# Delta-rule tiles in a pool of their own, three early expert loads, and transposes one chunk later

## The chip, the cores and the metric

The kernel runs on one core of a Trainium2 chip. The metric is the device time of one execution in microseconds (us). Five engines work from queues of their own, each in the order that was fixed when the program was built: TensorE (PE: matmuls and transposes), VectorE (DVE), ScalarE (ACT), GpSimd (POOL) and SyncE (SP, which issues all loads of weights). They meet at semaphores: an instruction waits until what it reads is there and what it overwrites is no longer used.

## The reference

Two layers over 256 tokens of width 1024, in fp32. Each layer has a mixer of three branches, whose outputs are joined and projected back, and a feed-forward part, dense in layer 0 and a mixture of experts in layer 1:

```python
for layer in range(DEPTH):                     # 2
    h = rmsnorm(x, mix_norm[layer])
    (c_q, c_kv, k_rope, lru_x, lru_gate, g_q, g_k, g_v, g_z, g_a, g_b) = jnp.split(h @ w_in[layer], split_at, axis=-1)
    y_mla = mla_mixer(...)      # 4 heads, attention by chunks, causal over chunks of 64
    y_lru = rglru_mixer(...)    # gated linear recurrence, 512 channels
    y_gdn = gdn_mixer(...)      # gated delta rule, 4 heads of 128, chunks of 64 with a triangular solve
    x = x + jnp.concatenate([y_mla, y_lru, y_gdn], axis=-1) @ w_out[layer]
    h = rmsnorm(x, ffn_norm[layer])
    if layer % 2 == 0:
        x = x + swiglu(h, ...)                 # width 2816
    else:
        x = x + moe_swiglu(h, ...)             # 8 experts of width 3584, the best 2 for each token
```

## The kernel before, in words

**Precision.** A weight is split into a high part `h` (a copy on ACT, line 271) and a low part `l` (the difference on DVE, line 272), and a product is three matmuls: high by high, high by low, low by high (`mm3`). All matmuls and transposes are issued by one helper, line 119, so that the profile tells them apart by the tiles: `mm` are projections, `gd` products of the mixers, `tp` transposes, `gu` the experts' gate and up products, `py` their down products. Inverse square roots are an addition on DVE (line 195) and a power on POOL (line 196).

**The mixer.** `mixer(l)` holds one generator for each part of the work: `gdn_in` and `gdn` (delta rule), `lru_in` and `lru_out`, `mla_in`, `mla_qkv` (queries, keys, values), `attn`, `zgate`, `gdn_out`, `wo0` to `wo2` (output projection, added into the residual at line 485). A table written by hand, `PLAN`, says in which order they advance by a step; a step with `!` is pinned ahead of what follows. A scheduler then orders each engine's instructions within these bounds, by what is free and ready in its own model. All tiles of the mixer come from one pool, `mix`, which is closed by the step `free`, near the end of the table. The delta rule's tiles are `cb` (convolution input), `v2k`, `aad` and `aao` (decay masks), `nbm`, `p128` and the small `qi`, `pi`, `vi`; `cb` and `p128` are cleared by memsets on POOL (lines 517 and 611). The last reader of the masks is the matmul `gd<-g2k,aad`.

**The loads.** `load` issues one transfer of 1 MB on SP. Its buffer comes from a ring of 128 x 2048 tiles: five in the pool `rawp` and, in layer 1 from `free` on, six in a second one, `raw2`. While the string `HEAD` lasts, a load takes its place from there: one letter a load, `2` the second pool, `1` the first, `h`, `q` and `g` tiles that at this time lie idle (high and low parts, hidden tiles). `rawi` counts on around the ring; its starting value says which buffer is taken first when the string is used up:

```python
HEAD = "hhq222222111ggg11"
...
raw_pools[:] = ring2
rawi[0] = len(ring2)
head[:] = () if again else list(HEAD)
```

**The experts.** After the routing, tokens are gathered into slots: five experts have 64 slots (narrow: raw fp32 matmuls, no split) and three have 128 (wide: split weights). Each has seven groups of 512 hidden channels, and a group has four loads of gate and up weights (`mgu`) and two of down weights (`mdn`). Groups are chained in software: while the `gu` products of one group run, the hidden tile of the group before (`esg`: SiLU on ACT, line 1369, times up on DVE, line 1370) is transposed (`tp`) and multiplied down (`py`). Narrow and wide groups alternate over long stretches, and in nine narrow groups the transposes of the own hidden tile stand directly behind the 32 `gu` matmuls, ahead of `py`. A narrow group multiplies four chunks of eight matmuls; in `gate_up` the function `mid` issues the transposes after the second.

## Time and profile before

| what | value |
|---|---|
| median of three runs | 1464.56 us |
| lowest, highest | 1463.25, 1467.42 us |
| profiled execution, time | 1467.6 us |
| its span in the trace | 1465.8 us |
| mean granted TensorE clock | 0.986 |
| layer 0: mixer, dense part | 0 to 200, 200 to 411 us |
| layer 1: mixer, routing, experts | 411 to 614, 614 to 631, 631 to 1466 us |

The profiled execution is one run by itself: what lies around its span is 1.8 us, and it is 3.0 us over the median, so differences of durations in the trace are set against its own time and then carried to the median. A row of the timeline gives the start, the length, the engine, the line, the operation, what it writes and reads, and in brackets how long its engine stood idle ahead of it and what ended that. `x4` joins four such instructions in one row.

### The profile page before, as it was taken

How to read it: one execution, taken by the hardware profiler on the slowest of the kernel's cores; microseconds unless marked ns; L12 is line 12 of the kernel's file. 1: busy time of each engine (PE TensorE's matmuls, PEld its weight loads, DVE VectorE, ACT ScalarE, POOL GpSimd, SP SyncE). 2: the span in 40 equal slices, each digit the busy share in tenths (PEclk: the TensorE clock that was granted, in tenths of full speed). 3: DMA queues.
4: the chain of work that ended last, by engine and by line, in shares of the span. 5: the costliest groups of instructions: out<-in, count | busy, mean ns of one | idle time of the engine just before them, and what ended most of it. 6: DMA issues, size and time to landing. Idle time of an engine off the chain costs nothing.

```text
span 1465.8 us, 25644 instructions
## 1 busy us (share of the span) xinstructions
PE 1407.3 (96%) x10407; PEld 1093.5 (75%) x10407; DVE 842.4 (57%) x1250; ACT 680.7 (46%) x1059; POOL 98.2 (7%) x122
## 2 busy tenths in 40 slices
PE   6989999999999999999999999999999999999996
PEld 6988799999999887966666666656665656666663
DVE  7898676666568985644353535454534545364542
ACT  5655654444456657354352535243533434343430
POOL 1111201221011121000000000000000000000000
PEclk9999999999999999999999999999999999999998
DMA  6422336544544132889999999999999999999993
GB/s 247 146 88 101 116 115 231 175 174 159 187 173 173 60 115 102 347 347 391 425 426 426 425 426 425 426 425 426 426 425 421 424 422 426 425 409 426 425 426 156
DMA packets 63773, 442.96 MB, mean 302 GB/s; under 512 B 7200, under 2 KB 7456, under 8 KB 11936
## 3 DMA queue, kind: packets, MB, share of 16 engines
q1 hardware_dynamic: 63360, 441.01, 74.6%
q8 instruction: 83, 1.36, 0.4%
q10 hardware_dynamic: 288, 0.25, 0.1%
q14 instruction: 42, 0.34, 0.1%
HBM read 440.18 MB, written 1.05 MB: 301 GB/s over the span
## 4 chain that ended last, share of the span: by engine, by line
PE 87%; DVE 7%; issue 2%; ACT 2%; POOL 1%; DMA 0%; POOLq 0%; DVEq 0%; ACTq 0%
PE gu L119 34%; PE mm L119 19%; PE py L119 17%; PE gd L119 11%; PE tp L119 7%; DVE l L272 2%; DVE red L369 1%; POOL so L196 0%; ACT h L271 0%; DVE xl L350 0%; DMA raw<-prm 0%; DVE esg L1370 0%; ACT esg L1369 0%; DVE acc L1437 0%; ACT m4k L759 0%
## 5 line engine op out<-in xcount | busy, mean ns | idle before, releaser
L272 DVE TENSOR_TENSOR l<-raw,h 128x1024 fp32r<-128x1024 f32 x416 | 491.8, 1217 | 101.2 <-ACT h L271 100.0
L271 ACT ACTIVATE h<-raw 128x1024 fp32r<-128x1024 f32 x416 | 421.1, 1048 | 169.9 <-PE mm L119 81.0
L119 PE MATMUL gu<-raw,y 128*64 128x256 f32 x2160 | 251.9, 382 | 0.0
L119 PE MATMUL gu<-h,y 128*128 128x512 f32 (+1 forms) x704 | 222.0, 401 | 0.0
L119 PEld LDWEIGHTS gu<-raw,y 128*64 128x64 f32 x2160 | 151.3, 137 | 87.3 <-issue 16.5
L119 PE MATMUL mm<-xh,h 128*128 128x256 f32 (+1 forms) x672 | 193.6, 288 | 9.3 <-ACT h L271 9.3
L119 PE MATMUL mm<-xh,l 128*128 128x256 f32 (+1 forms) x672 | 193.4, 288 | 0.8 <-DVE l L272 0.8
L119 PE MATMUL mm<-xl,h 128*128 128x256 f32 (+1 forms) x672 | 193.3, 288 | 0.2 <-issue 0.2
L119 PEld LDWEIGHTS gu<-h,y 128*128 128x128 f32 (+1 forms) x704 | 129.2, 187 | 38.7 <-ACT h L271 6.5
L119 PE MATMUL gu<-l,y 128*128 128x512 f32 (+1 forms) x368 | 137.3, 396 | 1.7 <-DVE l L272 1.7
L119 PEld LDWEIGHTS mm<-xh,h 128*128 128x128 f32 (+1 forms) x672 | 128.5, 191 | 10.2 <-ACT h L271 9.3
L119 PEld LDWEIGHTS mm<-xh,l 128*128 128x128 f32 (+1 forms) x672 | 128.5, 191 | 1.9 <-DVE l L272 1.3
L119 PEld LDWEIGHTS mm<-xl,h 128*128 128x128 f32 (+1 forms) x672 | 128.6, 191 | 1.4 <-issue 0.7
L119 PE MATMUL py<-raw,htn 128*64 128x512 f32 x552 | 126.7, 598 | 0.0
L1370 DVE SCALAR_TENSOR_TENSOR esg<-gu,rs,esg 128x256 f32<-128x256 f32 x35 | 16.9, 484 | 146.9 <-ACT esg L1369 146.9
L1396 ACT ACTIVATE hth<-tp 128x512 fp32r<-128x512 f32 x21 | 12.5, 597 | 189.3 <-PE tp L119 189.3
L119 PEld LDWEIGHTS py<-raw,htn 128*64 128x64 f32 x552 | 37.0, 136 | 68.5 <-issue 66.3
L1369 ACT ACTIVATE esg<-gu,rs 128x256 f32<-128x256 f32 x35 | 16.6, 474 | 150.9 <-PE gu L119 150.9
L119 PEld LDWEIGHTS gu<-l,y 128*128 128x128 f32 (+1 forms) x368 | 66.0, 186 | 18.6 <-DVE l L272 2.7
L119 PE MATMUL mm<-y,h 128*128 128x256 f32 x384 | 70.2, 284 | 0.0
L119 PE MATMUL py<-l,hth 128*128 128x512 f32 x168 | 68.5, 408 | 1.2 <-DVE l L272 1.2
L1383 DVE SCALAR_TENSOR_TENSOR esg<-gu,rs,esg 128x512 f32<-128x512 f32 x21 | 15.8, 750 | 91.0 <-PE gu L119 91.0
(391 smaller groups left out, 2057.1 us busy)
## 6 DMA issues: line engine op xcount, KB each, us to landing
raw<-mgu SPq DMA_DIRECT2D x219, 1024.0 KB, 13.0
raw<-mdn SPq DMA_DIRECT2D x110, 1024.0 KB, 12.6
raw<-win SPq DMA_DIRECT2D x29, 1024.0 KB, 4.9
raw<-dgu SPq DMA_DIRECT2D x22, 1024.0 KB, 4.9
raw<-wout SPq DMA_DIRECT2D x12, 1024.0 KB, 4.8
raw<-ddn SPq DMA_DIRECT2D x8, 1024.0 KB, 4.9
raw<-ddn SPq DMA_DIRECT2D x4, 768.0 KB, 4.2
raw<-uqn SPq DMA_DIRECT2D x2, 1024.0 KB, 4.8
```

The costliest lines, as they stand in the source:

```text
L119: i = f(*a, **k)
L271: SC.activation(h[:, c], w, AF.Copy)
L272: V.tensor_tensor(out=lo[:, c], in0=w, in1=h[:, c].bitcast(F32), op=ALU.subtract)
L369: V.tensor_reduce(out=red, in_=sqv.rearrange("p k t -> p t k"), axis=AX.X, op=ALU.add)
L1369: keep(SC.activation(sg, ps[:, :256], AF.Silu, scale=rs))
L1370: keep(V.scalar_tensor_tensor(sg, ps[:, 256:], rs, sg, ALU.mult, ALU.mult))
L1383: keep(V.scalar_tensor_tensor(sg, ps[1], rs, sg, ALU.mult, ALU.mult))
L1396: keep(SC.activation(hth, pt, AF.Copy))
```

## The change

Three edits, and the diff's core. First, the delta rule's tiles are taken from a pool of their own, `gdp`, on the right side of the on-chip memory. It is closed when the generator `gdn` ends, long before `free`. Second, in layer 1 the room is given at that moment to a pool `raw3` of three load buffers, and the first three loads of expert 0 are issued (`pre`); `raw2` has three buffers instead of six, the ring keeps its eleven and `HEAD` its seventeen loads in another order, and `rawi` starts so that the first three places behind the string are `rawp` buffers. Third, in a narrow group `mid` stands after the third chunk.

```diff
-RAW2 = 6
+RAW2 = 3
+RAW3 = 3
-HEAD = "hhq222222111ggg11"
+HEAD = "333222hqh111ggg11"
...
+        def open_raw3():
+
+            pools["3"] = top.enter_context(tc.tile_pool(name="raw3", bufs=RAW3, side="right")), "raw3"
+            head[:] = HEAD[:RAW3]
+            for hf in range(RAW3):
+                pre.append(load(A["mgu"][0, 0, hf // 2, hf % 2]))
+
...
-            ring2[:] = [(rawp, "raw") if x == "1" else (raw2, "raw2") for x in HEAD if x in "12"]
+            pools["2"] = raw2, "raw2"
+            ring2[:] = [pools[x] for x in HEAD if x in pools]
...
+                st_g = st.enter_context(ExitStack())
+                gdp = st_g.enter_context(tc.tile_pool(name=f"gdp{l}", bufs=1, side="right"))
+
...
-                        cb = mp.tile([P, 2, S + 3], F32, tag="cb", name=nm("cb"), bufs=2)
+                        cb = gdp.tile([P, 2, S + 3], F32, tag="cb", name=nm("cb"), bufs=2)
...
-                    aad = mk(mp, [P, NT, HEADS, 2, P], F32, "aad")
-                    aao = mk(mp, [P, HEADS, 2, P], F32, "aao")
+                    aad = mk(gdp, [P, NT, HEADS, 2, P], F32, "aad")
+                    aao = mk(gdp, [P, HEADS, 2, P], F32, "aao")
...
-                    P128 = mk(mp, [P, NS, P], F32, "p128")
+                    P128 = mk(gdp, [P, NS, P], F32, "p128")
...
+                            if name == "gdn":
+                                st_g.close()
+                                if l == DEPTH - 1:
+                                    open_raw3()
...
-                        rawi[0] = len(ring2)
-
-                        head[:] = () if again else list(HEAD)
+                        rawi[0] = 2 * len(ring2) - sum(x in pools for x in head)
+
+                        head[:] = () if again else HEAD[RAW3:]
...
-                                    if m == 0:
-                                        mid()
+                                        if m > hf:
+                                            mid()
...
-                                for half in load(weights(name, i, *at), nk * cols, halves):
+                                for half in pre.pop(0) if pre else load(weights(name, i, *at), nk * cols, halves):
```

Since the tiles' places differ, the scheduler gives another order in layer 1's mixer too, though `PLAN` is the same. In the rows below, a tile's number is its running number in the program.

**PE at the end of the attention (585 to 593 us).** Here `t2k_7063` (`t2k_7080` after the change) is the attention's output, whose four transposes follow a chain over ACT, DVE and POOL; the last product ahead of that chain is `gd_7054` (`gd_7071`). Before, the rows from that product on are these:

```order
L119 MATMUL gd_7054<-m4k_6533,m4k_6943 128x128
L119 MATMUL tp_7102<-cst_82,g2k_6124 128x128 x2
L119 MATMUL gd_7054<-m4k_6533,m4k_6943 128x128 x7
L119 MATMUL tp_7102<-cst_82,g2k_6124 128x128 x2
L119 MATMUL tp_7111<-cst_82,g2k_6145 128x128 x4
L119 MATMUL mm_7130<-y_6379,h_7122 128x256
```

and around the transposes:

```order
L119 MATMUL mm_7163<-y_6379,h_7126 128x256
L119 MATMUL mm_7163<-y_6378,l_7127 128x256
L119 MATMUL tp_7156<-cst_82,t2k_7063 128x128 x4
L119 MATMUL mm_7163<-y_6378,h_7126 128x256
L119 MATMUL mm_7163<-y_6379,h_7126 128x256
```

After the change the same two places read:

```order
L120 MATMUL gd_7071<-m4k_6550,m4k_6960 128x128
L120 MATMUL tp_7119<-cst_82,g2k_6131 128x128 x2
L120 MATMUL gd_7071<-m4k_6550,m4k_6960 128x128 x7
L120 MATMUL tp_7119<-cst_82,g2k_6131 128x128 x2
L120 MATMUL tp_7128<-cst_82,g2k_6152 128x128 x4
L120 MATMUL mm_7180<-y_6395,l_7144 128x256
```

```order
L120 MATMUL mm_7180<-y_6396,h_7143 128x256
L120 MATMUL mm_7180<-y_6395,l_7144 128x256
L120 MATMUL tp_7173<-cst_82,t2k_7080 128x128 x4
L120 MATMUL mm_7216<-y_6900,h_7208 128x256
L120 MATMUL mm_7242<-y_6900,h_7208 128x256
```

Between the last `tp` of `g2k` and the transposes of `t2k` stood 32 `mm` rows; now 13 stand there, and the other 19 behind the transposes.

**DVE at the same place.** `so` is the squares' sum, `g2k` the gated delta-rule output and `raw_83` the residual into which the output projection `mm` is added. Before:

```order
L1005 SCALAR_TENSOR_TENSOR g2k_7107<-tp_7102,raw_4222,m4k_6680 128x512
L1005 SCALAR_TENSOR_TENSOR g2k_7116<-tp_7111,raw_4222,m4k_6680 128x512
L272 TENSOR_TENSOR l_7192<-raw_7189,h_7191 128x1024
L195 TENSOR_SCALAR so_1006_7069<-so_1006_7069 128x1
L1007 TENSOR_TENSOR y_7075<-g2k_7107,y_7074 128x4x128
L974 SCALAR_TENSOR_TENSOR t2k_7063<-t2k_7063,so_1006_7069,raw_4222 128x512
L1007 TENSOR_TENSOR y_7075<-g2k_7116,y_7074 128x4x128
L485 TENSOR_TENSOR raw_83<-mm_7130,raw_83 128x512
```

After:

```order
L1018 SCALAR_TENSOR_TENSOR g2k_7124<-tp_7119,raw_4226,m4k_6697 128x512
L1018 SCALAR_TENSOR_TENSOR g2k_7133<-tp_7128,raw_4226,m4k_6697 128x512
L1020 TENSOR_TENSOR y_7092<-g2k_7124,y_7091 128x4x128
L498 TENSOR_TENSOR raw_83<-mm_7180,raw_83 128x512
L196 TENSOR_SCALAR so_1009_7086<-so_1009_7086 128x1
L1020 TENSOR_TENSOR y_7092<-g2k_7133,y_7091 128x4x128
L987 SCALAR_TENSOR_TENSOR t2k_7080<-t2k_7080,so_1009_7086,raw_4226 128x512
L282 TENSOR_TENSOR l_7213<-raw_7206,h_7212 128x1024
L282 TENSOR_TENSOR l_7271<-raw_7268,h_7270 128x1024
```

The split `l` that stood ahead of `so` stands behind `t2k` now, and an addition into `raw_83` and one `y` stand ahead of `so`.

**PE and DVE at the queries and keys (548 to 551 us).** `t2k_6663` (`t2k_6680`) is a normed query tile that is transposed, `h_6732` and `l_6733` (`h_6749`, `l_6750`) parts of the weight `ukv`, `n` the norms. PE before, and after:

```order
L119 MATMUL mm_6691<-xh_4892,l_6684 128x256
L119 MATMUL tp_6716<-cst_82,rp_6619 128x128 x2
L119 MATMUL gd_6740<-h_6732,y_6546 128x512
L119 MATMUL gd_6740<-l_6733,y_6546 128x512
L119 MATMUL gd_6740<-h_6732,y_6547 128x512
L119 MATMUL mm_6691<-xh_4892,h_6687 128x256
L119 MATMUL gd_6740<-h_6736,y_6546 128x512
L119 MATMUL mm_6691<-xl_4893,h_6687 128x256
L119 MATMUL tp_6720<-cst_82,t2k_6663 128x128 x4
```

```order
L120 MATMUL mm_6708<-xh_4899,l_6701 128x256
L120 MATMUL tp_6733<-cst_82,rp_6636 128x128 x2
L120 MATMUL gd_6757<-h_6749,y_6563 128x512
L120 MATMUL tp_6737<-cst_82,t2k_6680 128x128 x4
L120 MATMUL gd_6758<-h_6749,y_6563 128x512
L120 MATMUL gd_6808<-h_6749,y_6563 128x512
L120 MATMUL mm_6708<-xh_4899,h_6704 128x256
L120 MATMUL mm_6708<-xl_4900,h_6704 128x256
L120 MATMUL mm_6708<-xh_4899,l_6705 128x256
```

Three `gd` and two `mm` rows moved from ahead of the transposes of `t2k` to behind them. DVE before, and after:

```order
L877 TENSOR_TENSOR n_919_6651<-n_919_6651,n_920_6652 128x4
L195 TENSOR_SCALAR n_919_6651<-n_919_6651,rcq_905_6583 128x4
L272 TENSOR_TENSOR l_6733<-raw_6730,h_6732 128x1024
L879 TENSOR_SCALAR n_919_6651<-n_919_6651,rcq_6552 128x4
L420 TENSOR_TENSOR t2k_6663<-gd_6624,n_919_6651 128x512
L420 TENSOR_TENSOR rp_6665<-gd_6534,n_919_6651 128x256
```

```order
L890 TENSOR_TENSOR n_922_6668<-n_922_6668,n_923_6669 128x4
L196 TENSOR_SCALAR n_922_6668<-n_922_6668,rcq_908_6600 128x4
L892 TENSOR_SCALAR n_922_6668<-n_922_6668,rcq_6569 128x4
L433 TENSOR_TENSOR t2k_6680<-gd_6641,n_922_6668 128x512
L433 TENSOR_TENSOR rp_6682<-gd_6551,n_922_6668 128x256
L282 TENSOR_TENSOR l_6750<-raw_6747,h_6749 128x1024
```

The split `l` between the two last `n` steps moved behind `rp`.

**PE in a narrow group.** The place is one where the group before was narrow too, and its hidden tile `esg_7806` (`esg_7807`) is transposed. Before, and after:

```order
L119 MATMUL gu_7869<-raw_7862,y_7528 64x256 x8
L119 MATMUL gu_7869<-raw_7870,y_7528 64x256 x8
L119 MATMUL tp_7892<-cst_82,esg_7806 128x128 x2
L119 MATMUL gu_7869<-h_7880,y_7528 64x256 x4
L119 MATMUL gu_7869<-l_7881,y_7528 64x256 x4
L119 MATMUL gu_7869<-h_7897,y_7528 64x256 x4
L119 MATMUL gu_7869<-l_7898,y_7528 64x256 x4
L119 MATMUL py_1133_7855<-h_7909,htn_7895 64x512 x2
```

```order
L120 MATMUL gu_7880<-raw_7873,y_7545 64x256 x8
L120 MATMUL gu_7880<-raw_7881,y_7545 64x256 x8
L120 MATMUL gu_7880<-h_7891,y_7545 64x256 x4
L120 MATMUL gu_7880<-l_7892,y_7545 64x256 x4
L120 MATMUL tp_7915<-cst_82,esg_7807 128x128 x2
L120 MATMUL gu_7880<-h_7903,y_7545 64x256 x4
L120 MATMUL gu_7880<-l_7904,y_7545 64x256 x4
L120 MATMUL py_1133_7866<-h_7920,htn_7918 64x512 x2
```

The transposes moved from behind the second to behind the third chunk. In the nine groups with the transposes of the own hidden tile behind all four chunks nothing moved there: `tp` of that tile, then `py`, follow the last `gu` row in both.

**SP in layer 1.** The rows of the loads from the last `win` ahead of `ukv`, with the semaphores that they wait for. Before, and after:

```order
L258 DMA raw_6681<-win 128x2048 [waits DMAHW1_49,DVE_49,Activation_49]
L258 DMA raw_6730<-ukv 128x2048 [waits DMAHW2_49,DVE_49]
L258 DMA raw_6945<-win 128x2048 [waits DMAHW3_49,DVE_49]
L258 DMA raw_7018<-wout 128x2048 [waits DMAHW4_49,DVE_49]
L258 DMA raw_7120<-wout 128x2048 [waits DMAHW5_49,DVE_49]
L258 DMA raw_7189<-wout 128x2048 [waits DMAHW6_49,DVE_49]
L258 DMA raw_7251<-wout 128x2048 [waits DMAHW7_49,DVE_49]
L258 DMA raw_7313<-wout 128x2048 [waits DMAHW0_49,DVE_49]
L246 DMA h_7600<-mgu 128x1024 [waits DVE_49,PE_49,Pool_49]
```

```order
L268 DMA raw_6698<-win 128x2048 [waits DMAHW1_49,DVE_49,Activation_49]
L268 DMA raw_835_6158<-mgu 128x2048 [waits PE_49,Pool_49]
L268 DMA raw_836_6160<-mgu 128x2048
L268 DMA raw_837_6162<-mgu 128x2048
L268 DMA raw_6747<-ukv 128x2048 [waits DMAHW2_49,DVE_49]
L268 DMA raw_6962<-win 128x2048 [waits DMAHW3_49,DVE_49]
L268 DMA raw_7035<-wout 128x2048 [waits DMAHW4_49,DVE_49]
L268 DMA raw_7137<-wout 128x2048 [waits DMAHW0_49,DVE_49]
L268 DMA raw_7206<-wout 128x2048 [waits DMAHW1_49,DVE_49]
L268 DMA raw_7268<-wout 128x2048 [waits DMAHW5_49,DMAHW2_49,DVE_49]
L268 DMA raw_7330<-wout 128x2048 [waits DMAHW6_49,DMAHW3_49,DVE_49]
L268 DMA raw_1090_7633<-mgu 128x2048 [waits DVE_49,DMAHW7_49,PE_49,Activation_49]
```

The three loads `raw_835`, `raw_836` and `raw_837` of expert 0's weights stand ahead of `ukv` now, the first with a wait for PE and POOL.

**POOL in layer 0.** Layer 1's two `MEMSET cb` and its `MEMSET p` (lines 530 and 624 in the changed kernel) stand in layer 0 now, ahead of the two `so` powers of its delta rule; before, they stood at the start of layer 1.

## Rows read from the trace of the kernel before

**Rows 1.** The page, busy time, share of the span and instructions of PE.
```profile
PE 1407.3 (96%) x10407; PEld 1093.5 (75%) x10407; DVE 842.4 (57%) x1250; ACT 680.7 (46%) x1059; POOL 98.2 (7%) x122
```

**Rows 2.** Stages: length, busy per engine (instructions), granted clock, DMA share, GB/s.
```profile
411.00:614.00 203.00, 192.87 (x1984) 178.84 (x1984) 158.24 (x291) 123.07 (x237) 33.94 (x46) 0.98 0.43 152
700.00:1440.00 740.00, 725.89 (x4182) 473.32 (x4181) 350.98 (x369) 294.44 (x387) 0.00 (x0) 1.00 1.01 424
```

**Rows 3.** PE's waits from 700 us to the end: total, times, longest.
```profile
PE tp L119 <- DVE esg L1370: 9.9, 9, 1.1
PE gu L119 <- DVE l L272: 1.7, 2, 1.4
```

**Rows 4.** One window, the columns of rows 2.
```profile
680.00:690.00 10.00, 10.00 (x75) 5.39 (x76) 2.15 (x3) 2.28 (x3) 0.00 (x0) 1.00 0.78 299
```

**Rows 5.** Timeline, SyncE's queue: start, us, what was issued.
```profile
524.48 0.33 SPq L258 DMA_DIRECT2D raw<-win  x1
532.83 0.33 SPq L258 DMA_DIRECT2D raw<-ukv  x1
```

**Rows 6.** Timeline of the queries and keys: start, us, instruction, wait ahead.
```profile
547.84 1.22 DVE L272 TENSOR_TENSOR l<-raw,h 128x1024 fp32r<-128x1024 f32 x1
548.08 1.86 POOL L196 TENSOR_TENSOR n<-n,mhalf 128x4 f32<-128x4 f32 x1 [0.43 <-DVE n L195]
548.67 0.48 PE L119 MATMUL gd<-h,y 128*128 128x512 f32 x1
550.12 0.28 PE L119 MATMUL mm<-xl,h 128*128 128x256 f32 x1
551.08 0.63 PE L119 MATMUL tp<-cst,t2k 128*128 128x128 f32 x4 [0.68 <-DVE t2k L420]
555.37 1.02 POOL L911 TENSOR_TENSOR n<-n,mhalf 128x4 f32<-128x4 f32 x1 [0.39 <-DVE n L910]
```

**Rows 7.** Timeline of layer 0's delta rule, and layer 1's memsets.
```profile
129.50 0.39 PE L119 MATMUL gd<-g2k,aad 128*128 128x128 f32 x2
130.66 1.01 POOL L196 TENSOR_TENSOR so<-so,mhalf 128x4 f32<-128x4 f32 x1 [16.06 <-DVE so L195]
131.70 0.16 DVE L723 TENSOR_TENSOR so<-so,rqs 128x4 f32<-128x4 f32 x1 [0.47 <-POOL so L196]
139.27 0.39 PE L119 MATMUL gd<-l,y 128*128 128x256 f32 x1 [0.90 <-DVE l L272]
411.81 0.15 POOL L517 MEMSET cb<- 128x6 f32 x2 [60.91 <-PE gd L119]
411.92 0.97 POOL L611 MEMSET p<- 128x1024 f32 x1
```

**Rows 8.** Timeline of the attention's end.
```profile
585.48 1.77 PE L119 MATMUL gd<-m4k,m4k 128*128 128x128 f32 x14
588.83 1.21 DVE L272 TENSOR_TENSOR l<-raw,h 128x1024 fp32r<-128x1024 f32 x1
589.96 0.14 DVE L195 TENSOR_SCALAR so<-so 128x1 f32<-128x1 f32 x1
590.19 0.93 POOL L196 TENSOR_TENSOR so<-so,mhalf 128x1 f32<-128x1 f32 x1 [12.27 <-DVE so L195]
591.15 0.75 DVE L974 SCALAR_TENSOR_TENSOR t2k<-t2k,so,raw 128x512 f32<-128x512 f32 x1 [0.45 <-POOL so L196]
592.05 0.63 PE L119 MATMUL tp<-cst,t2k 128*128 128x128 f32 x4 [0.32 <-DVE t2k L974]
```

**Rows 9.** The chain that ended last: start, us, what.
```profile
602.42 6.01 PE mm L119 x48
```

**Rows 10.** Windows ahead of the experts, the columns of rows 2.
```profile
145.00:150.00 5.00, 2.98 (x26) 2.77 (x25) 4.41 (x9) 3.22 (x5) 2.90 (x3) 1.00 0.09 21
225.00:230.00 5.00, 3.17 (x16) 3.17 (x17) 4.05 (x4) 1.06 (x1) 0.00 (x0) 0.71 1.02 406
230.00:235.00 5.00, 5.00 (x42) 5.00 (x42) 1.39 (x2) 2.08 (x2) 0.23 (x1) 0.95 0.78 256
```

More of the change, by code (lines that the diff above doesn't have):

```diff
@@ L223, in open_raw2 @@
             hl2.append(top.enter_context(tc.tile_pool(name="hl2", bufs=HL2)))
-            ring2[:] = [(rawp, "raw") if x == "1" else (raw2, "raw2") for x in HEAD if x in "12"]
-        ring2, early, loaded = [], [], []
+            pools["2"] = raw2, "raw2"
+            ring2[:] = [pools[x] for x in HEAD if x in pools]
+        ring2, early, loaded, pre = [], [], [], []
+        pools = {"1": (rawp, "raw")}
         hl_pools, hli = [hlp], [0]
@@ L234, in load @@
         def load(src, n=2048, halves=False):
-            kind = head.pop(0) if head else "1"
-            if kind not in "12":
+            kind = head.pop(0) if head else None
+            if kind and kind not in pools:
                 if kind in "hg":
@@ L248, in load @@
                 return [bufs[:m], bufs[m:]]
-            pool, tag = raw_pools[rawi[0] % len(raw_pools)]
+            pool, tag = pools[kind] if kind else raw_pools[rawi[0] % len(raw_pools)]
             rawi[0] += 1
@@ L529, in gdn_in @@
                         else:
-                            t = b2k([P, 2, S], "v2k", bufs=2)
+                            t = gdp.tile([P, 2, S], F32, tag="v2k", name=nm("v2k"), bufs=2)
                             SC.activation(t, co, AF.Silu)
@@ L604, in nbm @@
                     def nbm(m):
-                        t = mp.tile([P, NS, 32], F32, tag="nbm", name=nm("nbm"), bufs=2)
+                        t = gdp.tile([P, NS, 32], F32, tag="nbm", name=nm("nbm"), bufs=2)
                         G.tensor_tensor(out=t, in0=bc(nbs, [P, NS, 32], 2), in1=bc(lev[:, m], [P, NS, 32], 1),
@@ L615, in small_t @@
                     def small_t(tag, dt=F32):
-                        return mp.tile([P, NS, 32], dt, tag=tag, name=nm(tag), bufs=1)
+                        return gdp.tile([P, NS, 32], dt, tag=tag, name=nm(tag), bufs=1)
                     def quad(x, b):
```

## The prediction

> **What bounds the kernel now.** I read the page first, then the busy time by stage, then what TensorE (PE) waits for in each stage, and last the timeline around the places where the order of instructions changes. PE is busy for 1407.3 us, 96% of the span [rows 1], so some 58 us are left, and an edit that takes no work from PE can win at most what lies in those. By stage [rows 2], the experts (631 us to the end) hold more than half of the time: from 700 to 1440 us PE is busy for 725.9 of 740 us, while the DMA share is 1.01, at 424 GB/s. Two resources are full there at once, and the question is which of them sets the pace. The waits decide it: in this stage PE's largest wait is for VectorE's `esg`, nine times 1.1 us [rows 3]; a wait of PE for a transfer does not stand in that list. From 680 to 690 us the DMA share falls to 0.78 while PE is full [rows 4]: the transfers pause, because no buffer is free, not because PE is behind them. So from then on the transfers follow PE: a buffer comes free when PE has used it. I take PE as the bound. Layer 1's mixer, 411 to 614 us, is another matter: PE is idle for 10.1 of 203 us and the DMA share is 0.43 [rows 2]. Whatever the change gives or takes, it does so in that stage, by short chains over four engines.
>
> **The change, part by part.**
>
> *Early weights.* Three 1 MB loads of expert 0 move ahead of layer 1's `ukv` and `wout` loads. At 424 GB/s one takes 1.049/0.424 = 2.47 us, all three 7.4 us. They can start when the delta rule's tiles are free; in the order they stand directly behind the last `win` load before `ukv`, which was issued at 524.48 us, and `ukv` itself at 532.83 us [rows 5]. There are 8.35 us between the two and DMA is used to less than half in that stage [rows 2], so the 7.4 us fit and `ukv` is at most slightly late: its first use on VectorE, a split, is at 547.84 us [rows 6], 15 us behind its issue. What do the early loads give? The experts begin at 631 us, 90 us later, and PE waits for no load in their steady part [rows 3]. I put them at 0. What covers them is the pause of the transfers at 680 us: each MB that has come earlier only makes that pause longer. If the cover is not there, that is, if the transfers did set the pace, the gain is the whole 7.4 us; that is the lower bound. The upper one is on the other side: the first loads behind the head now go into the three oldest buffers instead of the six of the second pool, so one may be issued half a load later than before: half of 2.47 is 1.2 us, my estimate.
>
> *Transposes behind the third chunk.* In a 64-slot group the transposes of the previous hidden tile move eight matmuls later. Nothing is added; they wait less for VectorE, if they wait at all. The nine waits of 1.1 us [rows 3] do not stand there: they are at groups whose transposes are of their own hidden tile, behind all 32 `gu` rows, and these rows are the same in both orders. So 0; if I read these places wrongly, all nine may go: −9.9.
>
> *The memsets.* With a pool of their own, layer 1's `cb` and `p128` tiles stand where layer 0's stood, so their memsets are put on GpSimd's (POOL's) queue in layer 0, directly ahead of a `so` power. They must wait for the last reader of layer 0's tiles, which is PE's `gd<-g2k,aad` at 129.50 + 0.39 = 129.89 us; the memsets take 0.97 us and 0.15 [rows 7]. So the `so` power can start at 129.89 + 1.12 = 131.0 instead of 130.66 us at the earliest. DVE already waits for it there, 0.47 us [rows 7], and everything behind on DVE's queue moves with it, up to the split for which PE waits 0.90 us at 139.27 [rows 7]. At most 0.5, with some 0.15 for the semaphores between them; at least nothing, if a shorter wait elsewhere takes it up. I take 0.4, the difference of the two starts, because that wait of PE is behind the same queue.
>
> *Queries and keys, 548 to 558 us.* PE now reaches the transposes of `t2k` with one `gd` matmul ahead of them instead of four and two `mm`. The first `gd` ends at 548.67 + 0.48 = 549.15, the last `mm` at 550.12 + 0.28 = 550.40 [rows 6], so PE is there 1.25 us sooner. On DVE the split `l` that stood between the two `n` steps is gone from there. That split shortens the chain: POOL's power takes 1.86 us beside a split and 1.02 alone [rows 6], so 0.84 us come back. PE waits 0.68 us for these transposes now [rows 6]; after, 0.68 + 1.25 − 0.84 = 1.1. The work taken from ahead stands behind, so the net is the 0.4 by which the wait grows, and a tenth for the transposes of `rp` behind: +0.5. Bounds: −0.5 if the shorter chain reaches further (the later waits in this stretch shrink), +1.9 if the power stays at 1.86 (0.5 + 0.84) and half of a split of 1.22 us falls in front of a later wait (0.6).
>
> *The end of the attention, 585 to 593 us.* This is the largest term. After the last `gd<-m4k,m4k` a chain runs over ACT (`t2k`, then its squares), DVE `so` at 589.96, POOL 0.93 us, DVE `t2k` 0.75 us, then PE's four transposes at 592.05 us [rows 8]. The matmuls end at 585.48 + 1.77 = 587.25; the chain is 4.80 us long. Before, PE has the `tp<-cst,g2k` and 32 `mm` matmuls to do in this time and waits 0.32 us [rows 8]. After, only 13 `mm` stand there; the other 19 come behind. By the chain's row of 48 in 6.02 us [rows 9] one takes 0.125 us, so 19 are 2.4 us of cover less, and PE idles for 2.7 us instead of 0.32: **+2.4**. Below: the DVE split of 1.21 us at 588.83 [rows 8] is gone from the chain, which would take off up to 1.2: +1.2. Above: an addition of the output projection (DVE, 0.7 us by its like at 591.15 [rows 8]) now stands ahead of `so` on DVE: +3.1. Since the split ends only 0.08 us behind the start of `so` and ACT's part would be late anyway, I take the middle, 2.4.
>
> *Sum.* 0 + 0 + 0.4 + 0.5 + 2.4 = +3.3 us. The profiled execution of before took 1467.6 us, 1.8 more than its span, and lies 3.0 over the median of the three runs; so a profile after should show 1470.9 and the median goes to 1464.56 + 3.3 = **1467.9 us**. 0.3% is 4.4 us, about what a measurement of this kernel can tell from no change: under 1460.2 is faster, over 1468.95 slower.
>
> **The rivals.**
>
> *The clock falls in the new hole: slower.* PE's granted clock falls to the lower of its levels, 1.2 from 2.4 GHz, behind some idle stretches: from 225 to 230 us PE is busy for 3.17 us and the clock is 0.71, then 0.95 [rows 10]. In five-us windows that is 5 × 0.29 + 5 × 0.05 = 1.7 us lost. But from 145 to 150 us PE is busy for only 2.98 us, and the clock stays at 1.00 [rows 10]. Ahead of the experts I count nine such idle stretches; the clock fell behind five and stayed behind four, of which these are one each. A hole of 2.7 us is longer than that at 145 us, so it stands about even. With it: 3.3 + 1.7 = +5.0, 1469.6 us. It decides from 1.1 us on, the distance from 1467.9 to the bound.
>
> *DMA sets the pace of the experts: faster.* The share of 1.01 over 740 us [rows 2] speaks for it; that no wait for a transfer is among PE's waits [rows 3] and that the DMA paused at 680 us [rows 4] speak against. Then 7.4 us are won, and idle time of PE ahead of the experts costs nothing: 1457.2 us. The Trainium skill, Perfetto Trace Analysis, section Identifying the Most-Contended Engine, holds that matmul busy time is a poor measure of how near TensorE is to its limit, and that DMA is to be judged by how far HBM is used; by that rule the 96% of PE would prove nothing and DMA would be the bound of the experts. The waits of this trace don't agree with it.
>
> *The nine waits go after all: faster.* If the moved transposes free DVE or ACT at the right moment, half to all of 9.9 us could go: 1458.0 to 1462.9 us. The unchanged rows at those places speak against.
>
> *The ring makes PE wait: slower.* The three buffers taken first behind the head hold the second to fourth chunk of the first 128-slot expert. If they land late, up to three loads, 7.4 us, are added: 1475.3 us. Against it: the slack that the pause at 680 us shows [rows 4].
>
> *The order does not matter.* The 19 matmuls are only displaced, and if the chain at 585 us is short enough or the next stretch has idle time to give back, nothing is left: 1464.6 to 1466 us. Against it: PE waits for a chain there already, 0.32 us [rows 8], so the chain is no shorter than its present cover, and work that is moved behind a hole does not fill it.
>
> **How the numbers follow.** Hole without a fall of the clock 0.36 (1467.9); with it 0.32 (1469.6); nothing left 0.12; DMA 0.08; nine waits 0.06; ring 0.06. With bounds of its own, the likeliest runs from 1464.56 + 0.7 (0, −0.5, +1.2) to 1464.56 + 5.5 (0.5, 1.9, 3.1), 1465.3 to 1470.1. Slower: 0.32 less 0.06 of it that stays under the bound, 0.04 of the first that passes it, and the ring's 0.06, 0.36; I say 0.37. Faster: DMA and about half of the nine waits, 0.12 with rounding. Same: the rest, 0.51. The range takes in the likeliest's bounds, the clock's 1.7 and the ring's 1.2 above (1473.0), and below half of the nine waits' span, −6.9 + 3.3 (1461.0); the DMA, ring and rest of the nine are left out.
>
> **What would show it.** In the profile after: no wait of PE for a transfer in the experts, and the nine waits still there; a wait of PE at the last `tp<-cst,t2k`, around 590 us, of 1.5 to 3 us; the `so` power in layer 0 starting about 0.4 us later; POOL's `n` at 548 us near 1.0; and a clock of 1.00 from 590 to 600 us, or 0.7 to 0.9 if the rival holds. I am wrong if the experts' stage itself, 631 us to the end, is more than 2 us longer or shorter, or if PE's wait at the attention's end stays under 1 us.

## The result, and the profile after

The changed kernel takes 1473.95 us (median of 6 runs, 1472.03 to 1477.15) beside 1466.69 us of the kernel before on the same chip (6 runs, 1463.25 to 1468.4): ratio 1.0055 [1.0042, 1.0069] (in brackets a 95% interval), so it is slower: the medians lie 7.3 us apart, and by the ratio it is 8.1 us. In a later session, beside 20 runs of before, it was 1.0048 [1.0032, 1.0064], 7.0 us. Both ratios lie above the 1.003 from which the prediction calls it slower; its likeliest outcome was no change. The forecast was 1467.9 us, +3.3; the time lies 0.95 us above the range. The profiled execution of the changed kernel took 1475.98 us, its span is 1474.2 us: +8.4 against the span of before. The granted clock's mean is 0.986, as before.

The page, busy time of each engine with share and instructions (answers to [rows 1]); the work has not changed, the span has:

```profile
span 1474.2 us, 25638 instructions
PE 1406.8 (95%) x10407; PEld 1092.4 (74%) x10407; DVE 842.7 (57%) x1250; ACT 681.8 (46%) x1059; POOL 98.0 (7%) x122
```

Stages and windows of the changed kernel, columns as in [rows 2, 4]:

```profile
411.00:614.00 203.00, 187.45 (x1919) 173.13 (x1918) 153.55 (x286) 121.66 (x236) 32.67 (x43) 0.97 0.43 157
...
700.00:1440.00 740.00, 724.30 (x4171) 473.99 (x4170) 351.17 (x367) 299.31 (x390) 0.00 (x0) 1.00 1.01 423
...
595.00:600.00 5.00, 1.64 (x13) 1.23 (x11) 4.49 (x8) 4.02 (x7) 0.93 (x1) 1.00 0.00 0
600.00:605.00 5.00, 4.36 (x19) 4.06 (x20) 2.18 (x7) 0.10 (x1) 0.00 (x0) 0.52 0.88 320
605.00:610.00 5.00, 5.00 (x36) 5.00 (x36) 0.89 (x2) 1.03 (x2) 0.00 (x0) 0.79 1.02 424
...
660.00:670.00 10.00, 10.00 (x77) 5.51 (x78) 1.71 (x2) 1.18 (x3) 0.00 (x0) 1.00 0.32 111
```

From 411 to 614 us PE is busy for 187.45 us, 5.4 less than in [rows 2]: the stage has slipped, and fewer of its instructions (1919, not 1984) lie before 614. The experts' row is that of before within 1.6 us of 740. The five-us windows at 595 us show where: PE is busy for 1.64 of 5 us, and then works at half clock (0.52) for most of the next five.

PE's waits in the changed kernel, layer 1's mixer above and the experts (700 us to the end) below: total, times, longest (answers to [rows 3]):

```profile
PE tp L120 <- DVE t2k L987: 2.8, 1, 2.8
...
PE tp L120 <- DVE t2k L433: 1.9, 2, 1.2
PE tp L120 <- ACT t2k L431: 1.1, 2, 0.8
...
PE tp L120 <- POOL rp L864: 1.1, 1, 1.1
...
PE tp L120 <- DVE esg L1387: 9.9, 9, 1.1
PE tp L120 <- ACT h L1446: 2.8, 4, 0.7
PE py L120 <- DVE l L282: 2.4, 4, 1.2
PE gu L120 <- DVE l L282: 1.7, 2, 1.3
```

The nine waits are as long as before, and a transfer is again not in the list. The largest of the mixer is the one forecast, at the attention's last transposes. The timeline of the changed kernel at the three places of the prediction, and SyncE's queue (answers to [rows 5 to 8]):

```profile
130.80 0.15 POOL L530 MEMSET cb<- 128x6 f32 x2 [15.70 <-DVE y L821]
130.87 0.96 POOL L624 MEMSET p<- 128x1024 f32 x1
131.93 1.01 POOL L197 TENSOR_TENSOR so<-so,mhalf 128x4 f32<-128x4 f32 x1
132.97 0.17 DVE L736 TENSOR_TENSOR so<-so,rqs 128x4 f32<-128x4 f32 x1 [1.03 <-POOL so L197]
...
526.43 1.29 SPq L268 DMA_DIRECT2D raw<-mgu  x3
533.74 0.33 SPq L268 DMA_DIRECT2D raw<-ukv  x1
...
548.91 1.02 POOL L197 TENSOR_TENSOR n<-n,mhalf 128x4 f32<-128x4 f32 x1 [0.43 <-DVE n L196]
551.13 0.63 PE L120 MATMUL tp<-cst,t2k 128*128 128x128 f32 x4 [1.17 <-DVE t2k L433]
555.03 0.44 PE L120 MATMUL tp<-cst,rp 128*128 128x128 f32 x2 [1.05 <-POOL rp L864]
...
592.05 1.77 PE L120 MATMUL gd<-m4k,m4k 128*128 128x128 f32 x14
595.73 0.28 PE L120 MATMUL mm<-y,l 128*128 128x256 f32 x1
596.76 0.14 DVE L196 TENSOR_SCALAR so<-so 128x1 f32<-128x1 f32 x1
596.98 0.93 POOL L197 TENSOR_TENSOR so<-so,mhalf 128x1 f32<-128x1 f32 x1 [13.90 <-DVE so L196]
597.94 0.75 DVE L987 SCALAR_TENSOR_TENSOR t2k<-t2k,so,raw 128x512 f32<-128x512 f32 x1 [0.45 <-POOL so L197]
598.61 2.35 DVE L282 TENSOR_TENSOR l<-raw,h 128x1024 fp32r<-128x1024 f32 x2
598.84 0.63 PE L120 MATMUL tp<-cst,t2k 128*128 128x128 f32 x4 [2.83 <-DVE t2k L987]
599.51 0.60 ACT L995 ACTIVATE y<-tp 128x512 fp32r<-128x512 f32 x1 [0.98 <-PE tp L120]
600.16 0.98 PE L120 MATMUL mm<-y,h 128*128 128x256 f32 x3 [0.69 <-ACT y L995]
600.88 0.68 DVE L996 TENSOR_TENSOR y<-tp,y 128x512 fp32r<-128x512 f32 x1
601.62 0.58 PE L120 MATMUL mm<-y,h 128*128 128x256 f32 x1 [0.49 <-DVE y L996]
```

Read the last block from below. The matmuls before the hole end at 596.01 us; the chain over ACT, DVE and POOL brings `t2k` at 598.69, so PE waits 2.83 us. Then it has the four transposes to do and nothing else: the next `mm` reads `y`, the copy of their result on ACT (0.69 us more), and the one after that the other half of `y`, which stands on DVE behind two splits of together 2.35 us (0.49 more). The three make 4.0 us, against 0.32 before [rows 8]: +3.7. The text ahead of the prediction is wrong here: the 19 matmuls that no longer stand between are not behind the transposes. Of the 47 `mm` of this stretch before had 32 between the `tp` of `g2k` and the transposes of `t2k` and 15 behind; now 34 stand ahead of the attention's last product, 13 between, and none behind.

By the same PE instructions in the two traces, the changed kernel is later by 0.8 us from the start (no edit lies there), +0.45 from the memsets, +1.4 at the queries and keys (549 to 562 us), +7.0 from 586 to 598 us (3.7 of waits, and 3.4 from 6.8 us at half clock), −1.2 in the routing (3.4 us at half clock instead of 6.8), +0.6 at 692, −1.6 at 966 (a fall of the clock that is missing) and +1.2 at 1427 us.

### The profile page after: what moved, and what is told of

Same layout as the page of the kernel before. It is cut to its first block, busy times and chain, and to the rows that moved or that the text cites. A ratio compares the mean times of both kernels' runs of the same rounds, so it can differ in the third digit from the quotient of the medians.

```text
span 1474.2 us, 25638 instructions
## 1 busy us (share of the span) xinstructions
PE 1406.8 (95%) x10407; PEld 1092.4 (74%) x10407; DVE 842.7 (57%) x1250; ACT 681.8 (46%) x1059; POOL 98.0 (7%) x122
## 3 DMA queue, kind: packets, MB, share of 16 engines
HBM read 440.18 MB, written 1.05 MB: 299 GB/s over the span
## 4 chain that ended last, share of the span: by engine, by line
PE 80%; DVE 8%; DMA 6%; ACT 2%; issue 2%; POOL 1%; POOLq 0%; SPq 0%; DVEq 0%; ACTq 0%
PE gu L120 30%; PE mm L120 19%; PE py L120 15%; PE gd L120 10%; PE tp L120 6%; DMA raw<-mdn 3%; DMA raw<-mgu 3%; DVE l L282 2%; DVE red L379 1%; ACT h L281 1%; POOL so L197 0%; DVE xl L360 0%; DMA raw<-prm 0%; DVE acc L1454 0%; ACT m4k L772 0%
## 5 line engine op out<-in xcount | busy, mean ns | idle before, releaser
L120 PEld LDWEIGHTS gu<-l,y 128*128 128x128 f32 (+1 forms) x360 | 65.1, 185 | 17.9 <-DVE l L282 2.9
L120 PE MATMUL py<-h,htl 128*128 128x512 f32 x168 | 67.2, 400 | 0.0
## 6 DMA issues: line engine op xcount, KB each, us to landing
raw<-mgu SPq DMA_DIRECT2D x220, 1024.0 KB, 16.6
```

Source lines behind the costliest of these rows:

```text
L120: i = f(*a, **k)
```

## The experiments

Two theories. **Hole**: the change costs what PE newly waits, most of it at the attention's end; the cause is the scheduler's new order, not the transfers. **Clock** (rival): the waits are short, and the time goes because the clock falls behind them. Other suspects: the third edit, the place of the early loads, the transfers as the bound. A ratio stands for a kernel against before on the same chip; 0.001 is 1.5 us.

**The order at the attention's end, undone alone.** The changed kernel, with one step of `PLAN` advanced:

```diff
-mla_qkv! mla_qkv mla_qkv attn attn! attn attn! mla_qkv attn! zgate attn attn! zgate attn! attn zgate
+mla_qkv! mla_qkv mla_qkv attn attn! attn attn! mla_qkv attn! zgate attn attn! attn! zgate attn zgate
```

> The changed kernel with two neighbouring steps of layer 1's hand-written order exchanged (a pinned attention step ahead of a gate step), which puts 32 projection matmuls ahead of the attention's last transposes and 16 behind them, as before the change (13 and none after it); the three early loads, the memsets, the queries' and keys' rows and the experts stay as changed. Theory 1, the loss is the hole at the attention's end (waits of 2.83, 0.69 and 0.49 us) and the 6.8 us at half clock behind it: about 7 us come back, 1466 to 1468.5 us, the wait at the last transposes is under 1 us and the granted clock there 1.00. Theory 2, the loss is spread over the early loads, the ring and the experts, and the hole is made up for later: at most 2 us come back, 1472 to 1474 us.

Measured: 1470.44 us, 1.0030 [1.0019, 1.0042]; the clock is 1.00 from 590 to 610 us. The wait at the last transposes is gone; 1.4 us of shorter ones come instead (0.62 for `m4k`, 0.46 for `so`, 0.16 for `y`, 0.2 for a split). So of the 7.0 to 8.1 us the hole is 2.6 to 3.7, with an interval of some ±2.7 us; the traced waits give 4.0 − 1.4 = 2.6. The rest, 4.4 us, lies elsewhere; the time falls between what the two theories had.

```profile
590.00:610.00 20.00, 19.23 (x157) 18.59 (x156) 15.32 (x24) 9.10 (x15) 0.93 (x1) 1.00 0.75 289
```

**The early loads issued later.** The changed kernel, but a step `raw3` of the table, behind the one that loads `ukv`, opens the pool and issues the three loads:

```diff
-mla_qkv! mla_qkv mla_qkv attn attn! attn attn!
+mla_qkv! mla_qkv raw3 mla_qkv attn attn! attn attn!
...
-                                if l == DEPTH - 1:
-                                    open_raw3()
```

> The changed kernel with the three early loads issued behind the load of ukv and ahead of the second layer's attention, instead of at the end of the delta rule; pools, ring, memsets and the transposes in the experts as changed. In this order the rows of layer 1's mixer on TensorE are again those of before. Theory 1, the early loads cost time only because they stand ahead of ukv in the queue and so change the order of the mixer: everything but the memsets' 0.4 us comes back, 1466.5 to 1468 us. Theory 2, the loads themselves or the ring cost: 1470 to 1474 us. If the early loads were worth their 7.4 us of transfer time in the experts, they would be so here: about 1459.5 us.

Measured: 1468.4 us, 1.0018 [1.0009, 1.0027]. Its one wait at the attention's last transposes, and SyncE's queue:

```profile
PE tp L120 <- DVE t2k L987: 0.3, 1, 0.3
...
523.86 0.81 SPq L268 DMA_DIRECT2D raw<-mgu  x2
531.18 0.33 SPq L268 DMA_DIRECT2D raw<-ukv  x1
531.56 0.42 SPq L268 DMA_DIRECT2D raw<-mgu  x1
```

The edit does less than its expectation says: the scheduler still puts two of the three loads ahead of `ukv`, and only the third comes behind it. That is enough to give the mixer the order of before on PE (32 matmuls between, 15 behind), and the hole is gone. The loads still come some 70 us ahead of the experts; between the routing and the end this kernel and the one with the third edit alone (below) differ by 0.2 us. So the early weights and the ring win nothing, as forecast, but the order that the scheduler makes with *all three loads ahead of `ukv`* costs: this kernel against the changed one, 4.4 to 5.5 us, and 4.1 without the third edit, each with an interval of 2.4 to 2.9 us to either side. The traced waits of the two places that its order undoes, 3.7 + 1.4, make 5.1. It is not that `ukv` comes late: in the changed kernel it is issued at 533.74 us, 0.9 later than in [rows 5], which is no more than the offset that the kernel has by then. The order can be read from a program without a run: with the pools alone, too, it is that of before up to the experts.

**The hole filled.** 32 matmuls without use, into a tile that is then overwritten, ahead of the last transposes of the changed kernel:

```diff
                         pt = mk(ptp, [P, HEADS, P], F32, "tp")
+                        for _ in range(32 if l and t else 0):
+                            T.matmul(pt[:, 0:2], lhsT=lh[:, 0, :P], rhs=lh[:, 0], start=True, stop=True)
```

> The changed kernel with 32 matmuls of no use (128x256, about 0.12 us each) ahead of the attention's last four transposes in layer 1, into the tile that the transposes then overwrite; nine projection matmuls that stood ahead of the transposes come to stand behind them. The chain that the transposes wait for stays. Theory 1a, the half clock behind the hole is what idling costs: TensorE works through the hole, the granted clock stays at 1.00 from 600 to 610 us, and 3 to 3.4 us come back, 1470.5 to 1471.5 us, though no useful work was moved. Theory 1b, the clock falls for another reason (the transfers that start there, the kind of matmuls): the clock still falls and the time is that of the changed kernel or up to 0.5 us more, 1474 to 1474.5 us.

Measured: 1473.6 us, 1.0051 [1.0034, 1.0068]. Its windows:

```profile
595.00:600.00 5.00, 5.00 (x43) 4.87 (x43) 3.15 (x7) 2.19 (x7) 0.56 (x1) 1.00 0.01 3
600.00:605.00 5.00, 4.89 (x41) 4.68 (x40) 4.14 (x9) 2.45 (x3) 0.00 (x0) 1.00 0.75 285
...
614.00:640.00 26.00, 24.97 (x180) 24.14 (x180) 15.47 (x60) 10.34 (x26) 0.70 (x1) 0.80 0.94 373
```

The filling kept the clock at 1.00, and from the transposes to the routing it takes 21.8 us instead of 24.7, 2.9 us less. The order differs too: nine projection matmuls (about 1.1 us) came from ahead of the transposes to behind them, where they fill the waits of 0.69 and 0.49 us. The two about cancel, so 2.9 us is near the local price of the half clock. But the whole time is that of the changed kernel, and the clock falls elsewhere: in the routing (0.80 over 26 us, 0.93 in the changed kernel). So what was won from the clock at this place was not won in the sum.

**The third edit alone, and left out.** Before with `mid` moved, and the changed kernel with `mid` where it was:

```diff
-                                    if m == 0:
-                                        mid()
+                                        if m > hf:
+                                            mid()
```

> The kernel of before with the third edit alone: the transposes in narrow groups behind the third chunk. Both theories say no difference, within 1 us of before, and the nine waits of 1.1 us for esg are still there. If the waits went, up to 9.9 us less.

> The changed kernel with the transposes of narrow groups back behind the second chunk; early loads, pools, ring and the order of layer 1's mixer as changed. The third edit alone made before 2.7 us slower on the mean, of which the profiles show 0.6 us as a longer wait of TensorE near 692 us; the rest stood in longer stretches at half clock at the routing. Theory 1, only the 0.6 us belong to the edit and the rest is where the clock's grid happened to fall: 1473 to 1474 us, and the wait for l at the first wide down product is 0.6 us shorter. Theory 2, the whole 2.7 us belong to the edit: 1471 to 1471.7 us.

Alone: 1468.35 us, 1.0020 [1.0010, 1.0030]. Left out: 1471.82 us, 1.0038 [1.0022, 1.0053], so 1.4 to 2.5 us better than the changed kernel, within the intervals. Alone, the edit misses its forecast of 1 us: it isn't free. In the trace of the edit alone I find 0.6 of its 2.9 us, where down products wait for a split:

```profile
689.29 0.50 PE L119 MATMUL py<-l,hth 128*128 128x512 f32 x1 [0.34 <-DVE l L272]
...
PE tp L119 <- DVE esg L1370: 8.8, 8, 1.1
...
PE py L119 <- DVE l L272: 1.6, 2, 1.2
PE tp L119 <- DMA raw<-mgu: 1.1, 1, 1.1
```

Before waits 1.2 us for this split, in one place. The nine waits stay; one of them is now put down to a load that came as late as `esg`. The other 2.3 us of this kernel are not found in waits. Part of them stands in the clock: what the clock takes from a run (worked out at the end of this section) is on the mean 22.4 us in its ten runs and 20.3 in the 29 of before beside them.

**Both without the third edit.** The late loads, and the swapped step, each with `mid` where it was:

> The kernel with the early loads behind ukv (mixer rows as before the change), and the transposes of narrow groups behind the second chunk: what is left of the change are the pools, the memsets in layer 0, the early loads and the ring's order. Theory 1: before plus the memsets' 0.4 us, 1465.8 to 1466.5 us. Theory 2, the whole 2.7 us of the third edit are no chance: also about 1466 us, but then the changed kernel without that edit must be 2.7 us faster too. If the early loads or the ring cost anything: 1467 us or more; if the early loads gain their 7.4 us of transfers: 1458.5 us.

> The changed kernel with both the two exchanged steps (32 projection matmuls ahead of the attention's last transposes and 16 behind, instead of 13 and none) and the transposes of narrow groups back behind the second chunk; early loads ahead of ukv, pools, ring and queries' and keys' rows as changed. Against the changed kernel without the third edit (1471.75 us on the mean of 7) only the order at the attention's end differs. Theory 1a, the hole costs its idle time alone, 2.83 + 0.69 + 0.49 - 0.32 = 3.7 us, because stretches at half clock that follow it stand in for others elsewhere: 1468 us. Theory 1b, the hole costs its idle time and 3.4 us of half clock, 7 us: 1464.7 us. Theory 2, the hole is no cause: 1471 to 1472 us.

Late loads: 1467.89 us, 1.0010 [0.9997, 1.0022]: not told from before, though it lies where its expectation put a cost of the loads or the ring (1467 us or more). The trace has 0.5 us from the memsets, 0.9 from two waits at 1428 us, for the parts of the last wide down weights, and a wait for a load of expert weights into one of the idle tiles of `HEAD`, which the trace of the changed kernel does not have:

```profile
659.77 0.65 PE L120 MATMUL gu<-hth,y 128*64 128x256 f32 x4 [1.12 <-DMA hth<-mgu]
```

Swapped: 1468.5 us, 1.0027 [1.0015, 1.0040], where the theory of the idle time alone had 1468; here PE waits 0.4 us for the same load. So the new order of the loads can make PE wait a little, as the prediction's ring rival feared for other buffers. Beside these two the third edit is worth 1.2 and 0.4 us (0.0008 and 0.0003), less than alone; the hole, with `mid` left out of both, 1.6 us. Each of these differences has an interval of 2.3 to 2.9 us to either side, so none of them is told from nothing by itself.

**A fall of the clock, cured in before.** In before the clock falls at 421 us, in the norm ahead of layer 1. Useless matmuls of the unit matrix are put into the two holes (`warm` is set in layer 1 alone):

```diff
+            for _ in range(12 if warm else 0):
+                T.matmul(ps[:, :P], lhsT=ident, rhs=ident, start=True, stop=True)
...
+            for _ in range(8 if warm else 0):
+                T.matmul(psb[:, :P], lhsT=ident, rhs=ident, start=True, stop=True)
```

> The kernel of before with 12 and 8 matmuls of no use (128x128 fp32, 0.13 us each) put into the two waits of TensorE for the norm of layer 1's mixer, 1.67 us before 418.43 and 1.06 us before 421.23, into tiles that are overwritten next. Theory 1, the clock falls behind such waits because TensorE idles: the fall at 421.7 us, which all profiles so far have there, is gone, stage 411 to 430 us is 1.7 us shorter, and the time goes to about 1464 us. Theory 2, the clock falls for another reason or falls elsewhere instead: no gain, 1465.5 us, and a fall near that place stays.

Measured: 1466.5 us, 1.0003 [0.9987, 1.0020]. The clock stays up (before: 0.91 from 411 to 430 us):

```profile
411.00:430.00 19.00, 17.90 (x155) 17.71 (x154) 14.93 (x21) 9.58 (x14) 2.29 (x5) 1.00 0.60 225
...
410.34 2.84 PE L119 MATMUL tp<-cst 128*128 128x128 f32 x24
```

The fillers were too long: 2.84 and 1.95 us for holes of 1.67 and 1.06, for one of them took 0.24 us and not the 0.13 expected; and a wait of 1.10 us for the norm stays behind the first. The 3.2 us over are more than the 1.7 that the clock gives back (0.09 of 19 us), so this run can't tell what a cheaper cure would bring.

**Are the transfers the bound of the experts?** Before, but each load of the experts moves half of its chunk, and the half is read twice (half of the expert weights are left out):

```diff
+                if len(raw_pools) > 1:
+                    loaded[:] = [SY.dma_start(t[:, :n // 2], src[:, :n // 2])]
+                    return [[t[:, :n // 2]]] * 2
```

> The kernel of before in which the steady loads of the experts move only the first half of each 1 MB chunk and the matmuls read it twice: the transfers of the experts are halved, the instructions on TensorE stay. Theory 1, TensorE is the bound of the experts: DMA share near 0.5 from 700 us on, the experts' 826 us the same within 2 us. Rival, the transfers set the pace there: the experts get shorter by far more than 10 us.

Measured: 1445.55 us, 0.9862 [0.9839, 0.9886]:

```profile
700.00:1420.00 720.00, 719.68 (x4179) 470.85 (x4179) 354.96 (x368) 307.45 (x387) 0.00 (x0) 1.00 0.64 217
```

The size is what the rival forecast (far more than 10 us), but not by its mechanism: in before, none of PE's waits in this stage is for a transfer. PE's work is as before and now fills the stage; the nine waits are gone, and with them the places where they stood. The scheduler, which reckons with loads of half the length, gives another order: the transposes of the own hidden tile behind the `gu` rows, nine places in before, are none here. The waits that went add up to 14.9 us (9.9 for `esg`, 2.1 of the 2.8 for `h`, 1.7 and 1.2 for `l`); the rest of the 20 is not assigned. So the transfers seem to cost time here by the order that was made for them; no run has the new order with whole loads, or the old one with halves, so the two are not told apart. That bears on a rule that the prediction used: the Trainium skill, Perfetto Trace Analysis, section Identifying the Most-Contended Engine, holds matmul busy time to be a poor measure of how near PE is to its limit. Here it was a fair one: of 740 us PE was busy for 725.89 [rows 2], and about the 14 us that this leaves idle could go. The rival that the prediction made of the page's DMA rule did not come true: early loads won nothing.

**More cover than before.** Before, with one step of the output projection two places earlier, so that 45 `mm` stand ahead of the attention's last transposes and none behind:

```diff
-        zgate wo1 attn gdn_out! wo1 gdn_out! gdn_out wo1 attn! wo1 wo0 wo0 wo0 wo0 wo2! wo2 wo1 wo2! free
+        zgate wo1 attn wo1 gdn_out! wo1 gdn_out! gdn_out wo1 attn! wo0 wo0 wo0 wo0 wo2! wo2 wo1 wo2! free
```

> The kernel of before with one step of the hand-written order moved: the last group of the output projection's first part stands two steps earlier. 24 projection matmuls stand between the delta rule's output transposes and the attention's last transposes, 45 in all behind the attention's product, and none behind these transposes, where 15 stood. So the wait ahead of them stays small, but TensorE comes to the next projection with nothing to do until the transposes are copied and split. Theory 1, the second half of the hole (0.69 + 0.49 us in the changed kernel) is made by what stands behind the transposes: such waits show, 1 to 1.3 us, time +1.2 us, about 1467 us. If that is followed by a fall of the clock and this costs: +2.9, 1468.7 us. Theory 2, work moved ahead of a chain is as good a cover as behind it: no difference, 1465.8 us.

Measured: 1462.68 us, 0.9980 [0.9966, 0.9995]: against every theory 2.9 us faster than before, and the fastest kernel here that does the whole work. The wait ahead of `mm` came (1.82 us, more than expected), but the clock behind it did not fall, nor did it in the routing:

```profile
593.94 1.11 PE L119 MATMUL mm<-y,h 128*128 128x256 f32 x4 [1.82 <-ACT y L982]
...
590.00:595.00 5.00, 3.07 (x23) 2.63 (x23) 4.96 (x8) 3.64 (x5) 0.00 (x0) 1.00 0.29 91
595.00:600.00 5.00, 5.00 (x44) 5.00 (x43) 2.05 (x7) 0.36 (x1) 0.00 (x0) 1.00 0.87 306
612.00:628.00 16.00, 14.69 (x132) 14.45 (x131) 9.14 (x32) 6.14 (x13) 0.00 (x0) 1.00 1.01 424
```

At this place PE is idle for longer than before and the kernel is faster: the gain is in the clock. Why it stayed up is not shown.

**The two kernels again.** The changed kernel and before, unaltered, for a second trace of each:

> The changed kernel once more, for a second trace. Theory 1a, the half clock behind the hole comes and goes with where the hole falls, and what is lost to the clock over the whole execution is as in before, 20 to 21 us; idle 4.0 us at the attention's end again. Theory 1b: 6.8 us at half clock right behind the hole again, and more lost to the clock than before.

> The kernel of before once more, for a second trace. If the lengths at half clock in the routing (6.8 us in the first trace of before, 13.7 us in those with the third edit alone, the late loads and the filled hole) are chance, this one may show any of 3.4 to 13.7 us; if they belong to the edits, 6.8 us.

Changed: 1472.07 us, 1.0048 [1.0032, 1.0064]; its profiled run took 1468.2 us. Before, one run: 1464.61 us. Windows of the changed kernel, then in a fence of its own one of before:

```profile
590.00:595.00 5.00, 1.71 (x7) 1.14 (x7) 4.55 (x7) 2.80 (x4) 0.93 (x1) 0.79 0.18 29
595.00:600.00 5.00, 4.71 (x23) 4.71 (x24) 0.85 (x6) 0.00 (x0) 0.00 (x0) 0.52 0.98 395
```

```profile
612.00:632.00 20.00, 19.38 (x117) 18.21 (x118) 11.24 (x56) 10.34 (x26) 0.70 (x1) 0.65 1.02 419
```

The hole of the changed kernel repeats: 2.83, 0.69 and 0.39 us of waits, and 6.8 us at half clock. But in this trace its routing has no half clock, while before has 17.1 us of it there (6.8 in the first trace). What the clock takes from a run, its span times (1 − mean granted clock), is on the mean 20.1 to 21.1 us for before, 20.6 and 17.6 for the changed kernel in its two sessions, 20.6 with the swapped step, 23.3 with the hole filled, 17.9 with the filled norm and 13.2 for the kernel with more cover. So the changed kernel loses no more to the clock than before, as far as its ten runs tell; its fall behind the hole stands in for falls elsewhere. In the 73 runs of before that stand beside the experiments, time and this loss rise together (correlation 0.88), 0.58 us of time for each us lost. By this estimate the 7 us less of the kernel with more cover are worth 4.1 us, more than the 2.9 that it gained, so that its order by itself would be about 1.2 us slower, as its expectation had it; and the 2.1 us more of the third edit alone are 1.2 of its 2.9. With this part taken out of every run, the changed kernel is still 8.5 and 7.5 us slower than before in its two sessions (±1.5 and ±1.0), and 4.5 (±0.7) with the swapped step: its loss is not the clock's. What is left is idle time: 0.45 + 1.4 + 3.7 + 0.6 = 6.1 us, with the 1.2 at 1427 us 7.3, beside 7.0 to 8.1 measured. That last wait, for parts of the last wide down weights, is in both traces of the changed kernel (0.9 and 1.8 us) and in the three changed kernels without the third edit, but not in those with the swapped step or the late loads that keep this edit; its cause was not tried.

## Why the prediction was wrong, step by step

- **Sign and place: right.** The loss is at the attention's end, and the early weights give nothing. No transfer is waited for, and the nine waits have not moved. The transfers pause earlier and longer: in the changed kernel their share is 0.32 at 660 us. From 640 to 690 us the shares leave 13.9 us idle, 6.3 before, and the difference, 7.6 us, is the 7.4 of the three loads: the lead was given back whole.
- **Memsets: right.** 0.4 forecast, 0.45 measured; DVE's wait behind the power grew from 0.47 to 1.03 us.
- **Queries and keys: within its bounds.** The chain did as it was worked out (the power 1.02 us, the wait 1.17 against 1.1), but the wait for `rp` behind, 1.05 us, was put at a tenth: +1.4 against +0.5.
- **The end of the attention: the step that failed.** "19 are 2.4 us of cover less" was right for the first wait: 2.83 − 0.32 is 2.5. But the term stopped there. What stands *behind* the transposes was taken for independent work; it reads their result, and the splits that left the chain's head now stand ahead of `y`. +2.4 was forecast, 3.7 measured. The row behind the transposes, `mm_7216<-y_6900`, stood in the order ahead of the prediction, with a tile's number that was not followed.
- **Transposes behind the third chunk: 0 forecast, not 0.** 0.6 us are traced (a split that PE now reaches too early), 2.9 are measured for the edit alone, 0.4 to 2.5 beside the others. By the estimate above some 1.2 us of the 2.9 are the clock's; what the remainder is stays open.
- **The clock rival: right in the profile, wrong in the sum.** The clock fell, 0.52 and 0.79 in two windows, at 3.4 us and not 1.7. Over whole runs the changed kernel loses no more to the clock than before, and the kernel with the hole filled is no faster.
- **The base.** The prediction started from 1464.56 us; before took 1466.69 in the session of the result. Of the 6.1 us between forecast and result 2.1 are this; without it the time would lie within the range, and the terms would still be 4.0 to 4.8 us short (3.3 forecast, 7.3 to 8.1 measured).

In short: a mechanism rightly named, one term too small by 1.3 us, a second by 0.9, a third taken for nothing (0.6, perhaps more), and the +1.2 at the end of the experts, which was not thought of. Two slips of the prediction played no part: the chain of 48 took 6.01 us in [rows 9], not 6.02, and the −6.9 us of the range's lower end is not worked out.

## What to carry to other kernels

When cover is taken from a chain, price both sides of the waiting instruction: count what is ready ahead of it, and follow by the tiles' numbers whether what stands behind it can run before its result is back. A load put ahead of another can cost without being late, if a scheduler makes the order with it in mind: compare the orders before the transfers, on SyncE's queue too, for the step of a table need not be where a load is issued. Judge an edit by whole runs as well as by the place, since time won back from the clock at one place may be lost at another.

## What was not expected of the hardware

- The clock falls in stretches where PE is busy nearly throughout. In before's second trace it is 0.65 over 20 us of routing with PE busy for 19.38. The same instructions of the routing took 15.7 us in traces without a fall, 16.3 to 16.6 with 3.4 or 6.8 us at half clock, 18.2 with 13.7 and 19.2 with 17.1: 3.5 us between executions of an unchanged stage, in 14 traces.
- An idle 1.82 us of PE left the clock at 1.00 (more cover), and waits of 2.83, 0.69 and 0.4 to 0.5 us close together brought 6.8 us at half clock in all three traces that have them (the two of the changed kernel and the one of it without the third edit). Which idle time is answered by a fall could not be told from the length of the wait.
- Which fall a run gets moves its time by several us: the runs of the kernel with more cover lie between 1458.65 and 1467.78 us. Part of each ratio here is this. No experiment separates it; the estimate of 0.58 us for each us lost to the clock is worked out from runs of one kernel.
